# Four seven-product chunks instead of three in three feed-forward parts, and weights split 1024 columns at a time

## The chip, the cores and the metric

The kernel runs on one core of a Trainium2 chip. The metric is the time of one execution in device microseconds; lower is better. The core has five instruction streams that run side by side and meet through semaphores: PE (TensorE: matmuls and transposes), DVE (VectorE), ACT (ScalarE), POOL (GpSimd) and SP (SyncE, which issues the DMAs here). Each stream runs its instructions in the order of the program.

## The reference

The model is a trunk of two layers over 256 rows of width 1024. Every layer has a half-step feed-forward part, a mixer, and a second half-step feed-forward part:

```python
D_MODEL = 1024; SEQ = 256; DEPTH = 2; D_FF = 2816
def swiglu(h, w_gate, w_up, w_down):
    return (jax.nn.silu(h @ w_gate) * (h @ w_up)) @ w_down
for i in range(DEPTH):
    h = rmsnorm(x, ffn1_norm[i])
    x = x + 0.5 * swiglu(h, ffn1_w_gate[i], ffn1_w_up[i], ffn1_w_down[i])
    h = rmsnorm(x, mix_norm[i])
    proj = h @ w_in[i]          # q_s | k_s | v_s | q_m
    ...
    # i even: chunked attention with a relative bias; i odd: differential attention
    # with rotary q and k; both: cross attention into mem with 4 heads
    ...
    x = x + jnp.concatenate([o_s, o_m], axis=-1) @ w_out[i]
    h = rmsnorm(x, ffn2_norm[i])
    x = x + 0.5 * swiglu(h, ffn2_w_gate[i], ffn2_w_up[i], ffn2_w_down[i])
return x
```

All arrays are float32.

## The kernel before

The rows are two tiles of 128 (tb = 0 and 1). A float32 product is made of three matmuls on operands that were split in a high and a low piece: hi·hi, lo·hi and hi·lo. The function `dense` issues these three (L416, L419, L422), each with 128 rows and 512 columns.

The weights come in 164 chunks of 128x2048 float32, 1 MB each. `loader` (L281) issues their DMAs on SP's queue into three buffers called `raw`. `split_hi` (L321) makes the high piece on ACT by a cast, `hi<-raw`; `split_lo` (L340) makes the low piece on DVE by a subtraction, `lo<-raw,hi`. Both work on 512 columns in one instruction, so four instructions on each engine make a chunk. There are four hi and four lo buffers; a matmul that is done frees them.

The feed-forward part (`ffn`) has 11 groups of 256 hidden columns. Each group takes two chunks of gate and up weights into two PSUM banks `gu`. Then ACT applies silu (L526), DVE multiplies (L529) and transposes (L537, `hb`), a DMA writes that to DRAM (L543, `hd`) and another reads it back turned (L548, `hr`); ACT and DVE split it into `ht` (L557, L559). Then come 11 chunks of down weights, c = 0 to 10. Chunks 0 to 7 are used in turn. The last three (`SPLIT`) are used by quarters, first both column halves of the first row tile, then of the second; this is called the split run below. After each quarter `finish` adds the sum into x (L499), and PE's transposes (`xtp`), DVE and ACT make the next part's input from it (y L460, xh L463, xl L465).

In some down chunks the 8 block products of 128x128 by 128x512 are replaced by seven. The table `SEVEN` names them by layer and part: none in the first part of layer 0, chunks 1, 4, 6 in its second part and in the first part of layer 1, and 1, 4, 7 in the last. Such a chunk needs four sums of weight blocks on DVE (L334, `wsum`), seven splits instead of four on each engine, sums of the blocks of h (L573, `sf`) and their splits (L582 on ACT, L586 on DVE, `h7`), and four PSUM banks m1, m5, m6, m7, which are added up and put into x after the last such chunk (`seven_sums`: L617, L611, L606, `msum`). It spans two hi and two lo buffers. `seven_forms` of the third such chunk and of any later one waits in the plan until the second of them is at work.

The order of instructions on each engine is set when the program is written: `Flow` keeps a clock for each engine with a cost for each operation, and threads (loader, split_hi, split_lo, evac, ffn and so on) take their turn by that clock. `calm_a` and `calm_v` hold a split back until its engine is free in the plan. The chip sees only the resulting order and the semaphores.

In layer 1's mixer POOL and DVE share the rotary embedding: POOL multiplies by the sine table (L1038, two instructions), DVE by the cosine table (L1041, `m`) and DVE adds the two (L1045); PE then transposes the sum (`qktp`). Other names of the mixer: `pj` the input projection, `hss` and `v` sums of squares and their scaling, `qkn` the normed q and k, `pe` and `PT` the attention's weights, `oT` its output.

Of the kernel before, what the change touches and what calls it, by code (L numbers as in the profile page):

```python
# [12 lines left out]
F32 = mybir.dt.float32  # L13
# [7 lines left out]
P = 128  # L21
# [5 lines left out]
NG = FF // 256  # L27
# [115 lines left out]
def kernel(  # L143
# [96 lines left out]
    class Chunk:  # L240
        def __init__(self, parts):
            self.parts = parts
            self.raw = self.hi = self.lo = None
            self.arrive = self.early = None
            self.seven = False
            self.hit = [None] * 7
            self.lot = [None] * 7
            self.tt = [None] * 4
            self.uses = 0

        def part(self, lo, q):

            t = (self.lo if lo else self.hi)
            if self.seven:
                t, q = t[q // 4], q % 4
            return t[:, q * 512:(q + 1) * 512]

    chunks = []
# [5 lines left out]

    def add_chunk(parts, uses=8):
        c = Chunk(parts)
        c.uses = uses
        c.index = len(chunks)
        chunks.append(c)
        return c  # L270

    def loader():
        for i, c in enumerate(chunks):
            yield lambda: raw_left[0] > 0
            raw_left[0] -= 1
            c.raw = wraw.tile([P, 2048], F32, tag="raw", name=f"raw{i}")
            c.block = lambda q, c=c: c.raw[:, q * 512:(q + 1) * 512] if not c.seven else c.raw[:, (0, 2, 3)[q] * 512:
                                                                                          (1, 3, 4)[q] * 512]
# [26 lines left out]
    def split_hi():  # L305
        for i, c in enumerate(chunks):
            n = 2 if c.seven else 1
            yield lambda: c.raw is not None and hl_left[0] >= n
            hl_left[0] -= n
            yield c.early or c.arrive  # L310
            c.hi, c.lo = ([whl.tile([P, 2048], F32R, tag=x, name=f"{x}{i}_{j}") for j in range(n)] for x in ("hi", "lo"))
            if not c.seven:
                c.hi, c.lo = c.hi[0], c.lo[0]
            for q in range(7 if c.seven else 4):
                if q == 2:
                    yield c.arrive
                if c.seven and q >= 3:
                    yield lambda: c.tt[q - 3] is not None
                    yield c.tt[q - 3]
                yield calm_a(i)  # L320
                nc.scalar.copy(out=c.part(0, q), in_=c.block(q))  # L321
                c.hit[q] = flow.act(512)

    def split_lo():
        for i, c in enumerate(chunks):
            if c.seven:
                yield lambda: c.hi is not None and g2.left >= 6
                yield c.arrive
                r = [c.raw[:, q * 512:(q + 1) * 512] for q in range(4)]
                t = [g2.take([P, 512], F32, "wsum") for _ in range(4)]  # L330
                c.block = lambda q, r=r, t=t: ([r[0], r[2], r[3]] + t)[q]
                for j, x, y in ((0, r[1], r[0]), (1, r[3], t[0]), (2, r[3], r[1]), (3, r[2], t[1])):
                    yield calm_v(i)
                    nc.vector.tensor_sub(t[j], x, y)  # L334
                    c.tt[j] = flow.dve(512)
            for q in range(7 if c.seven else 4):
                yield lambda: c.hit[q] is not None
                yield c.hit[q]
                yield calm_v(i)
                nc.vector.tensor_sub(c.part(1, q), c.block(q), c.part(0, q).bitcast(F32))  # L340
                c.lot[q] = flow.dve(512)
                if q == 3:
                    raw_left[0] += 1
            if c.seven:
                g2.give(4)
# [16 lines left out]
    SEVEN = {(0, 1): (), (0, 2): (1, 4, 6), (1, 1): (1, 4, 6), (1, 2): (1, 4, 7)}  # L362
# [9 lines left out]

    def plan_ffn(l, nm, wg, wu, wd):
        gu = []
        for g in range(NG):
            ids = []
            for c in range(2):
                pieces = 2 if len(chunks) < 2 else 1
                a = cols4(wg[l], c, g * 256, 256, 0, pieces)
                b = cols4(wu[l], c, g * 256, 256, 256, pieces)  # L380
                ids.append(add_chunk([q for ab in zip(a, b) for q in ab]))
            gu.append(ids)
        plan[l, nm, "gu"] = gu
        dn = []
        for c in range(NG):
            dn.append(add_chunk(turned2(wd[l], c)))
            if c in SEVEN[l, nm]:
                dn[-1].seven, dn[-1].uses = True, 7
        plan[l, nm, "dn"] = dn
# [19 lines left out]
    def dense(ps, xh, xl, ready, c, need, sl, start, stop):  # L409
# [5 lines left out]
        wh, wl = (c.part(0, need), c.part(1, need)) if sl is None else (sl(c.hi), sl(c.lo))  # L415
        nc.tensor.matmul(out=ps, lhsT=xh, rhs=wh, start=start, stop=False)  # L416
        flow.pe(T_MM)
        flow.step()
        nc.tensor.matmul(out=ps, lhsT=xh, rhs=wl, start=False, stop=False)  # L419
        flow.pe(T_MM)  # L420
        flow.step()
        nc.tensor.matmul(out=ps, lhsT=xl, rhs=wh, start=False, stop=stop)  # L422
        c.uses -= 1
        if c.uses == 0:
            hl_left[0] += 2 if c.seven else 1
        return flow.pe(T_MM)
# [13 lines left out]
    class Xt:  # L440
        def __init__(self):
# [6 lines left out]
            self.done = [0, 0]  # L448

    def prep_half(xt, tb, hf, gc, wait=0.0):  # L450
# [15 lines left out]
        g2.give()  # L466
# [44 lines left out]
    def ffn(l, nm, xt, gc_next):  # L511
# [5 lines left out]
        def evac(g, ps, end):  # L517
# [3 lines left out]
            for tb in range(2):  # L521
# [11 lines left out]
                banks.give()  # L533
# [57 lines left out]
        def seven(c, ms):  # L591
# [3 lines left out]
            for q, j, m in ((0, 0, 0), (1, 1, None), (2, 6, None), (3, 3, 1), (4, 4, 2), (5, 5, 3), (6, 2, None)):  # L595
                ps = ms[m] if m is not None else acc.ps[q // 6][q // 2 % 2 if q < 6 else 0]
                t = dense(ps, ht[0][:, j], ht[1][:, j], lambda: htt[c], dn[c], q, None,
                          first and m is not None, last and m is not None)
# [41 lines left out]
        for g, ids in enumerate(plan[l, nm, "gu"]):  # L640
            flow.until(banks.has(2))
            ps = [bank(f"gu{tb}", (P, 512)) for tb in range(2)]
            end = [None, None]
            flow.spawn(evac(g, ps, end))
            order = [(tb, c) for tb in range(2) for c in range(2)] if g == 0 and (l, nm) != (0, 1) else \
                    [(tb, c) for c in range(2) for tb in range(2)]
            for tb, c in order:
                for k in range(4):
                    kk = 4 * c + k
                    t = dense(ps[tb], xt.h[tb][:, kk, :], xt.l[tb][:, kk, :], lambda: xt.t[tb][kk], ids[c], k,  # L650
                              lambda w: k4(w)[:, k, :], kk == 0, kk == KT - 1)
                if c == 1:
                    end[tb] = t
        flow.until(banks.has(4))
        acc = Acc()
        nxt = None if gc_next is None else Xt()
        dn = plan[l, nm, "dn"]

        def down(c, k, tb, hf):
# [4 lines left out]
                         lambda w: k2(w)[:, k, sl], c == 0 and k == 0, c == NG - 1 and k == 1)  # L664
# [145 lines left out]
    def memory_kv(l):  # L810
# [46 lines left out]
        for tb in range(2):  # L857
            for c in range(2):
                for k in range(4):
# [3 lines left out]
                              lambda w: k4(w)[:, k, :], kk == 0, kk == KT - 1)  # L863
# [117 lines left out]
    def mixer(l, xt, gc_next):  # L981
# [23 lines left out]
        def proj(i, evac):  # L1005
            flow.until(banks.has(2))
            ps = [bank(f"pj{tb}", (P, 512)) for tb in range(2)]
            for tb in range(2):
                for c in range(2):
                    for k in range(4):  # L1010
                        kk = 4 * c + k
                        t = dense(ps[tb], xt.h[tb][:, kk, :], xt.l[tb][:, kk, :], lambda: xt.t[tb][kk],
                                  plan[l, "in"][i][c], k, lambda w: k4(w)[:, k, :], kk == 0, kk == KT - 1)
# [357 lines left out]
        nxt = Xt()  # L1371
        ids = plan[l, "out"]

        def outp(i, k, tb, hf):
# [6 lines left out]
                         lambda w: k2(w)[:, k, sl], i == 0 and k == 0, i == 3 and k == 1)  # L1381
# [116 lines left out]
```

## Time and profile before

| | us |
|---|---|
| median of three executions | 964.88 |
| the three | 964.7, 964.88, 967.41 |
| the profiled execution | 964.95 |
| its span, first to last instruction | 963.2 |
| PE busy | 954.8 (99%) |
| DVE busy | 745.0 (77%) |
| ACT busy | 567.9 (59%) |
| POOL busy | 60.5 (6%) |

Rows of the profile give the line of the kernel (L340), the engine, the operation, what is written and read by the program's names (`lo<-raw,hi`), the shape, and how many. In the groups the numbers behind the bar are the busy time in us and the mean of one in ns, and behind the next bar the idle time just before them and what ended it. In a timeline the first number is the start in us and the second how long it took; in square brackets is the idle time before. PEld is the load of weights into the array, which overlaps PE. Matmuls overlap one another in the records, so that their rate is read from start to start.

### The profile page before, as it was taken

How to read it: one execution, taken by the hardware profiler on the slowest of the kernel's cores; microseconds unless marked ns; L12 is line 12 of the kernel's file. 1: busy time of each engine (PE TensorE's matmuls, PEld its weight loads, DVE VectorE, ACT ScalarE, POOL GpSimd, SP SyncE). 2: the span in 40 equal slices, each digit the busy share in tenths (PEclk: the TensorE clock that was granted, in tenths of full speed). 3: DMA queues.
4: the chain of work that ended last, by engine and by line, in shares of the span. 5: the costliest groups of instructions: out<-in, count | busy, mean ns of one | idle time of the engine just before them, and what ended most of it. 6: DMA issues, size and time to landing. Idle time of an engine off the chain costs nothing.

```text
span 963.2 us, 13464 instructions
## 1 busy us (share of the span) xinstructions
PE 954.8 (99%) x4525; PEld 783.9 (81%) x4525; DVE 745.0 (77%) x1569; ACT 567.9 (59%) x1215; POOL 60.5 (6%) x65
## 2 busy tenths in 40 slices
PE   8999999999999999999999999999999999999998
PEld 7888888888777888888888888888787788888886
DVE  6777777788777877759986775797989886776785
ACT  6655555666676655545645555565677765554551
POOL 0000000021210000000000000000343100000000
PEclk9999999999999999999999999999999999999999
DMA  8988877486525479766568777666641468777661
GB/s 282 328 267 285 250 263 246 145 272 208 176 88 175 154 224 284 235 229 205 184 208 254 247 245 220 212 202 219 207 143 44 134 196 283 232 254 225 215 190 44
DMA packets 169295, 204.04 MB, mean 212 GB/s; under 512 B 9673, under 2 KB 144394, under 8 KB 169226
## 3 DMA queue, kind: packets, MB, share of 16 engines
q1 hardware_dynamic: 169226, 203.18, 66.0%
q8 instruction: 35, 0.57, 0.2%
q14 instruction: 34, 0.28, 0.1%
HBM read 188.99 MB, written 14.16 MB: 211 GB/s over the span
## 4 chain that ended last, share of the span: by engine, by line
PE 94%; DVE 3%; ACT 1%; DMA 1%; SPq 0%; issue 0%; ACTq 0%
PE gu L422 17%; PE gu L416 17%; PE gu L419 17%; PE acc L416 9%; PE acc L422 9%; PE acc L419 9%; PE pj L422 3%; PE pj L416 3%; PE pj L419 3%; PE xtp L429 1%; PE ptp L429 1%; PE S L1139 1%; PE AV L1220 1%; PE m L422 1%; PE m L419 1%; PE m L416 1%
## 5 line engine op out<-in xcount | busy, mean ns | idle before, releaser
L340 DVE TENSOR_TENSOR lo<-raw,hi 128x512 fp32r<-128x512 f32 x647 | 413.7, 684 | 103.9 <-ACT hi L321 100.0
L321 ACT CAST hi<-raw 128x512 fp32r<-128x512 f32 x647 | 361.7, 618 | 219.0 <-PE gu L422 123.6
L422 PE MATMUL gu<-hi,xl 128*128 128x512 f32 x704 | 274.3, 390 | 0.0
L416 PE MATMUL gu<-hi,xh 128*128 128x512 f32 x704 | 274.1, 389 | 0.0
L419 PE MATMUL gu<-lo,xh 128*128 128x512 f32 x704 | 274.0, 389 | 0.0
L422 PEld LDWEIGHTS gu<-hi,xl 128*128 128x128 f32 x704 | 132.2, 188 | 27.4
L419 PEld LDWEIGHTS gu<-lo,xh 128*128 128x128 f32 x704 | 132.2, 188 | 27.3
L416 PEld LDWEIGHTS gu<-hi,xh 128*128 128x128 f32 x704 | 132.2, 188 | 27.3
L416 PE MATMUL acc<-hi,ht 128*128 128x512 f32 x280 | 109.6, 391 | 0.0
L422 PE MATMUL acc<-hi,ht 128*128 128x512 f32 x280 | 109.2, 390 | 0.0
L419 PE MATMUL acc<-lo,ht 128*128 128x512 f32 x280 | 109.1, 390 | 0.0
L422 PE MATMUL pj<-hi,xl 128*128 128x512 f32 x160 | 64.5, 403 | 0.0
L419 PE MATMUL pj<-lo,xh 128*128 128x512 f32 x160 | 63.6, 397 | 0.0
L416 PE MATMUL pj<-hi,xh 128*128 128x512 f32 x160 | 63.5, 397 | 0.0
L422 PEld LDWEIGHTS acc<-hi,ht 128*128 128x128 f32 x280 | 52.6, 188 | 11.0
L419 PEld LDWEIGHTS acc<-lo,ht 128*128 128x128 f32 x280 | 52.6, 188 | 10.7
L416 PEld LDWEIGHTS acc<-hi,ht 128*128 128x128 f32 x280 | 52.6, 188 | 10.7
L526 ACT ACTIVATE sil<-gu,xr 128x256 f32<-128x256 f32 x88 | 41.5, 472 | 28.6 <-PE gu L422 28.6
L559 DVE TENSOR_TENSOR ht<-hr,ht 128x512 fp32r<-128x512 f32 x35 | 24.1, 687 | 32.2 <-ACT ht L557 32.2
L529 DVE SCALAR_TENSOR_TENSOR h<-gu,xr,sil 128x256 f32<-128x256 f32 x88 | 42.2, 479 | 5.8 <-ACT sil L526 4.5
L557 ACT CAST ht<-hr 128x512 fp32r<-128x512 f32 x35 | 21.6, 618 | 41.9 <-DMA hr<-hd 41.8
L436 POOL TENSOR_TENSOR xr<-v,nhalf 128x1 f32<-128x1 f32 x12 | 8.4, 698 | 502.3 <-DVE v L434 502.3
(191 smaller groups left out, 1069.0 us busy)
## 6 DMA issues: line engine op xcount, KB each, us to landing
raw<-in_ffn_w_down_dram SPq DMA_DIRECT2D x176, 256.0 KB, 4.1
raw<-in_ffn_w_gate_dram SPq DMA_DIRECT2D x86, 512.0 KB, 4.3
raw<-in_ffn_w_up_dram SPq DMA_DIRECT2D x86, 512.0 KB, 5.5
raw<-in_w_in_dram SPq DMA_DIRECT2D x32, 512.0 KB, 4.1
hd<-hb SPq DMA_DIRECT2D x44, 256.0 KB, 2.3
hr<-hd SPq DMA_DIRECT2D x44, 256.0 KB, 5.3
raw<-in_w_out_dram SPq DMA_DIRECT2D x8, 1024.0 KB, 5.0
raw<-in_w_mem_kv_dram SPq DMA_DIRECT2D x4, 1024.0 KB, 5.4
```

Of the source, the lines that this page charges most:

```text
L321: nc.scalar.copy(out=c.part(0, q), in_=c.block(q))
L340: nc.vector.tensor_sub(c.part(1, q), c.block(q), c.part(0, q).bitcast(F32))
L416: nc.tensor.matmul(out=ps, lhsT=xh, rhs=wh, start=start, stop=False)
L419: nc.tensor.matmul(out=ps, lhsT=xh, rhs=wl, start=False, stop=False)
L422: nc.tensor.matmul(out=ps, lhsT=xl, rhs=wh, start=False, stop=stop)
L429: nc.tensor.transpose(out=dst, in_=src, identity=flip if flipped else ident)
L526: nc.scalar.activation(sil, ps[tb][:, 0:256], AF.Silu, scale=xt.r[tb])
L529: nc.vector.scalar_tensor_tensor(out=h, in0=ps[tb][:, 256:512], scalar=xt.r[tb], in1=sil, op0=ALU.mult, op1=ALU.mult)
L557: nc.scalar.copy(out=hi, in_=src)
L559: nc.vector.tensor_sub(lo, src, hi.bitcast(F32))
L1139: nc.tensor.matmul(out=ss[e][:, pr, :nk], lhsT=q[rows, pr, :], rhs=k[rows, pr, :], start=i == 0, stop=i == len(passes) - 1)
L1220: nc.tensor.matmul(out=av[64 * e:64 * e + 64, pr, :], lhsT=vsrc(kb, pr, e), rhs=pts[e][:, pr, kb, :], start=(kb == 0), stop=(kb == nb - 1))
```

## The change

Two things change. `SEVEN` becomes (1, 3, 5, 7) in the three parts that have such chunks. And a weight split takes 1024 columns at a time instead of 512, on ACT and on DVE, in all chunks but the first two. In a seven-product chunk one raw block is split alone (512), two that lie side by side together (1024), and the four sums alone (512 each). The sums no longer wait for a hi buffer in the plan, but for the raw chunk alone, and the raw buffer is given back in the plan after all splits of the chunk instead of after the fourth. For this the class `Chunk` is divided into a raw part and an `Item` that holds its splits as a list of units.

The changed kernel also has code for products of pairs of gate and up groups. Its table `PAIR` is None for every part, so this code issues nothing.

```diff
+    class Item:
+        def __init__(self, raws, uses=8):
...
+            w = 1 if len(items) < 2 else 2
+            self.units = [(self.own(q, w), q, w, None) for q in range(0, 4, w)]
...
     def split_hi():
...
-            for q in range(7 if c.seven else 4):
...
-                nc.scalar.copy(out=c.part(0, q), in_=c.block(q))
-                c.hit[q] = flow.act(512)
+            for src, q, w, dep in it.units:
...
+                nc.scalar.copy(out=it.part(0, q, w), in_=src())
+                t = flow.act(512 * w)
+                it.hit[q:q + w] = [t] * w
     def split_lo():
...
-                yield lambda: c.hi is not None and g2.left >= 6
-                yield c.arrive
...
+                yield lambda: all(r.raw is not None for r in it.raws) and g2.left >= it.takes + 2
+                yield max(r.arrive for r in it.raws)
...
-                nc.vector.tensor_sub(c.part(1, q), c.block(q), c.part(0, q).bitcast(F32))
-                c.lot[q] = flow.dve(512)
-                if q == 3:
-                    raw_left[0] += 1
+                nc.vector.tensor_sub(it.part(1, q, w), src(), it.part(0, q, w).bitcast(F32))
+                t = flow.dve(512 * w)
+                it.lot[q:q + w] = [t] * w
+            raw_left[0] += it.frees
...
-    SEVEN = {(0, 1): (), (0, 2): (1, 4, 6), (1, 1): (1, 4, 6), (1, 2): (1, 4, 7)}
+    SEVEN = {(0, 1): (), (0, 2): (1, 3, 5, 7), (1, 1): (1, 3, 5, 7), (1, 2): (1, 3, 5, 7)}
+    PAIR = {(0, 1): None, (0, 2): None, (1, 1): None, (1, 2): None}
...
+    def seven_item(it):
+        r = [it.own(q) for q in range(4)]
+        t = lambda j: lambda: it.t[j]
+        it.n, it.uses, it.takes, it.gives = 2, 7, 4, 4
+        it.sums = [(r[1], r[0]), (r[3], t(0)), (r[3], r[1]), (r[2], t(1))]
+        it.units = [(r[0], 0, 1, None), (it.own(2, 2), 1, 2, None)] + [(t(j), 3 + j, 1, j) for j in range(4)]
```

The order on three places follows. The number behind a name tells its chunk (76) and then a running number that differs between the two kernels; `x4` stands for four like instructions in a row.

DVE, in the down run of layer 0's second part, before: chunks 3 and 4 (76 and 77 in the program's count), where chunk 77 is a seven-product one, and the forms of the third such chunk.

```order
L340 TENSOR_TENSOR lo76_0_4540<-raw76_4356,hi76_0_4539 128x512 x4
L334 TENSOR_TENSOR wsum_4586<-raw77_4460 128x512
L334 TENSOR_TENSOR wsum_4587<-raw77_4460,wsum_4586 128x512
L334 TENSOR_TENSOR wsum_4588<-raw77_4460 128x512
L334 TENSOR_TENSOR wsum_4589<-raw77_4460,wsum_4587 128x512
L340 TENSOR_TENSOR lo77_0_4583<-raw77_4460,hi77_0_4581 128x512
L559 TENSOR_TENSOR ht_4601<-hr_4559,ht_4601 128x512
L340 TENSOR_TENSOR lo77_0_4583<-raw77_4460,hi77_0_4581 128x512 x2
L340 TENSOR_TENSOR lo77_0_4583<-wsum_4586,hi77_0_4581 128x512
```

The same place on DVE after the change, where chunk 76 is the seven-product one (`L344` is the split, `L657` a sum of blocks of h, `L670` its split); the rows begin with the last splits of its sums.

```order
L344 TENSOR_TENSOR lo76_1_4280<-wsum_4231,hi76_1_4278 128x512
L643 TENSOR_TENSOR ht_4300<-hr_4268,ht_4300 128x512
L657 TENSOR_TENSOR sf_4324<-hr_3789 128x128
L657 TENSOR_TENSOR sf_4324<-sf_4324,hr_3789 128x128
L657 TENSOR_TENSOR sf_4324<-hr_3789 128x128
L657 TENSOR_TENSOR sf_4324<-hr_3789,sf_4324 128x128
L657 TENSOR_TENSOR sf_4331<-hr_3981 128x128
L657 TENSOR_TENSOR sf_4331<-sf_4331,hr_3981 128x128
L657 TENSOR_TENSOR sf_4331<-hr_3981 128x128
L657 TENSOR_TENSOR sf_4331<-hr_3981,sf_4331 128x128
L344 TENSOR_TENSOR lo76_1_4280<-wsum_4232,hi76_1_4278 128x512
L670 TENSOR_TENSOR h7_4323<-hr_3789,h7_4322 128x256
```

The sums of blocks of h for the third and the fourth seven-product chunk now stand in one group ahead of the last split of chunk 76, and their splits behind it; before, one chunk's forms came at a time.

DVE, in the first part of layer 1, before: the end of the plain chunk 7 (113 in the program's count) and the last three, 114 to 116, with the sums of products (`L611`, `L606`) among them.

```order
L340 TENSOR_TENSOR lo113_0_6363<-raw113_6241,hi113_0_6362 128x512 x4
L340 TENSOR_TENSOR lo114_0_6388<-raw114_6279,hi114_0_6387 128x512 x4
L340 TENSOR_TENSOR lo115_0_6425<-raw115_6369,hi115_0_6424 128x512
L606 SCALAR_TENSOR_TENSOR x0_85<-msum_6431,x0_85 128x512
L611 TENSOR_TENSOR msum_6431<-msum_6431,m6_6157 128x512
L340 TENSOR_TENSOR lo115_0_6425<-raw115_6369,hi115_0_6424 128x512
L611 TENSOR_TENSOR msum_6432<-msum_6431,m5_6156 128x512
```

After the change (`L690` and `L695` are the sums), from the last split of chunk 113 on, which is now a seven-product one.

```order
L344 TENSOR_TENSOR lo113_1_5987<-wsum_5979,hi113_1_5985 128x512
L344 TENSOR_TENSOR lo114_0_6016<-raw114_5947,hi114_0_6015 128x1024 x2
L344 TENSOR_TENSOR lo115_0_6031<-raw115_5971,hi115_0_6030 128x1024 x2
L690 SCALAR_TENSOR_TENSOR x0_85<-msum_6073,x0_85 128x512
L695 TENSOR_TENSOR msum_6073<-msum_6073,m6_5762 128x512
L344 TENSOR_TENSOR lo116_0_6071<-raw116_6035,hi116_0_6070 128x1024
L695 TENSOR_TENSOR msum_6074<-msum_6073,m5_5761 128x512
L690 SCALAR_TENSOR_TENSOR x0_85<-msum_6074,x0_85 128x512
L344 TENSOR_TENSOR lo116_0_6071<-raw116_6035,hi116_0_6070 128x1024
```

The sums now stand among the splits of chunk 116, the last of the part, where they stood among those of chunk 115.

DVE, at the start of layer 1's mixer, before: the rotary embedding of the first block.

```order
L713 SCALAR_TENSOR_TENSOR qkn_6733<-pj0_6626,xr_6103,hf_6695 128x512
L340 TENSOR_TENSOR lo121_0_6708<-raw121_6623,hi121_0_6707 128x512
L1041 TENSOR_TENSOR m1_6757<-qkn_6733,ropeC_107 128x512
L340 TENSOR_TENSOR lo122_0_6737<-raw122_6663,hi122_0_6736 128x512
L707 TENSOR_REDUCE hss_6768<-sq_6746 128x8
L434 TENSOR_SCALAR v_6771<-hss_6768 128x8
L1045 TENSOR_TENSOR m1_6757<-m1_6757,m2_6756 128x512
L340 TENSOR_TENSOR lo122_0_6737<-raw122_6663,hi122_0_6736 128x512 x3
```

After the change (`L894` is qkn, `L1222` and `L1226` are the multiply and the add).

```order
L894 SCALAR_TENSOR_TENSOR qkn_6328<-pj0_6220,xr_5711,hf_6284 128x512
L344 TENSOR_TENSOR lo122_0_6321<-raw122_6248,hi122_0_6320 128x1024
L888 TENSOR_REDUCE hss_6342<-sq_6332 128x8
L514 TENSOR_SCALAR v_6345<-hss_6342 128x8
L1222 TENSOR_TENSOR m1_6348<-qkn_6328,ropeC_107 128x512
L1226 TENSOR_TENSOR m1_6348<-m1_6348,m2_6347 128x512
L344 TENSOR_TENSOR lo122_0_6321<-raw122_6248,hi122_0_6320 128x1024
L894 SCALAR_TENSOR_TENSOR qkn_6379<-pj1_6221,xr_5712,hf_6344 128x512
```

The split, the sum of squares and its scaling, which stood between the multiply and the add, now stand ahead of both.

Over the whole program the matmuls of 128x512 fall by 9, the splits `lo<-raw,hi` on DVE go from 647 of 512 columns to 20 of 512 and 312 of 1024, and the casts `hi<-raw` on ACT likewise; splits of weight sums go from 36 to 48 on each engine and the weight sums from 36 to 48. SP and POOL issue as many instructions as before; on SP some of the DMAs of `hd` and `hr` move past one or two loads of `raw`.

More of the change, by code (lines that the diff above doesn't have):

```diff
@@ L263, with add_raw @@
     at = [0]
+    def add_raw(parts):
+        chunks.append(Chunk(parts))
+        return chunks[-1]
     def add_chunk(parts, uses=8):
[L266 to L270, printed above, removed]
+        return Item([add_raw(parts)], uses)
     def loader():
@@ L305, in split_hi @@
     def split_hi():
[L306 to L313, printed above, removed]
-            for q in range(7 if c.seven else 4):
+        for i, it in enumerate(items):
+            yield lambda: hl_left[0] >= it.n and all(r.raw is not None for r in it.raws)
+            hl_left[0] -= it.n
+            yield max(r.early or r.arrive for r in it.raws)
+            it.hi, it.lo = ([whl.tile([P, 2048], F32R, tag=x, name=f"{x}{i}_{j}") for j in range(it.n)]
+                            for x in ("hi", "lo"))
+            for src, q, w, dep in it.units:
@@ L383, in plan_ffn @@
         plan[l, nm, "gu"] = gu
+        plan[l, nm, "work"] = [w for w in work if w not in ("11", "12", "22", "21")]
+        if pair is not None:
+            plan[l, nm, "pair"] = made
         dn = []
@@ L414, in dense @@
         at[0] = max(at[0], c.index)
-        wh, wl = (c.part(0, need), c.part(1, need)) if sl is None else (sl(c.hi), sl(c.lo))
+        wh, wl = c.part(0, need), c.part(1, need)
         nc.tensor.matmul(out=ps, lhsT=xh, rhs=wh, start=start, stop=False)
@@ L424, in dense @@
         if c.uses == 0:
-            hl_left[0] += 2 if c.seven else 1
+            hl_left[0] += c.n
         return flow.pe(T_MM)
@@ L465, in prep_half @@
         nc.vector.tensor_sub(xt.l[tb][:, ks, :], y, xt.h[tb].bitcast(F32)[:, ks, :])
-        g2.give()
+        if xt.keep:
+            xt.y[tb, hf] = y
+        else:
+            g2.give()
         t = flow.dve(512)
@@ L638, in seven_sums, with plain_chunk @@
             g2.give(2)
[L640 to L647, printed above, removed]
+        open_ = {}
+        def plain_chunk(g, c, tbs):
+            if g not in open_:
+                flow.until(banks.has(2))
+                open_[g] = [bank(f"gu{tb}", (P, 512)) for tb in range(2)], [None, None]
+                flow.spawn(evac(g, *open_[g]))
+            ps, end = open_[g]
+            for tb in tbs:
@@ new lines, in product @@
+        def product(m):
+            name, left = {"m1": ("b11", (0, 0)), "m5": ("t1", 0), "m7": ("t3", 2), "m6": ("t2", 1), "m3": ("b22", 3),
+                          "m2": ("b21", (0, 1)), "m4": ("t4", (1, 1))}[m]
+            flow.until(banks.has())
+            pb[m] = bank("pair_" + m, (P, 512))
+            if m == "m1":
+                flow.spawn(pair_sums())
+                for e in range(2):
+                    flow.spawn(evac(pair + e, pps[e], pend[e], (g2, g2)))
+            for k in range(4):
+                if isinstance(left, int):
+                    flow.until(lambda: xt.ft[left] is not None)
+                    f = xt.fm[left]
+                    fh, fl, ready = f[:, 0, k, :], f[:, 1, k, :], lambda: xt.ft[left]
+                else:
+                    tb, kk = left[0], 4 * left[1] + k
+                    fh, fl, ready = xt.h[tb][:, kk, :], xt.l[tb][:, kk, :], lambda: xt.t[tb][kk]
+                t = dense(pb[m], fh, fl, ready, pit[name], k, k == 0, k == 3)
+            mt[m] = t
+            if m == "m3":
+                g4.give(4)
@@ L654, in ffn @@
+        if pair is not None:
+            flow.spawn(pair_forms())
+        work = list(plan[l, nm, "work"])
+        if (l, nm) != (0, 1):
+            for tb in range(2):
+                for c in range(2):
+                    plain_chunk(0, c, (tb,))
+            work = work[2:]
+        for w in work:
+            if isinstance(w, str):
+                product(w)
+            else:
+                plain_chunk(*w, range(2))
         flow.until(banks.has(4))
         acc = Acc()
-        nxt = None if gc_next is None else Xt()
+        nxt = None if gc_next is None else Xt(nm == 2 and PAIR[l + 1, 1] is not None)
```

210 lines of the change are left out of this document (156 added, 54 removed).

## The prediction

> **What bounds the kernel now.** I read the page first (busy time, chain, groups), then the windows, the waits, and the timelines of the places that the change touches.
>
> ```profile
> span 963.2 us, 13464 instructions
> PE 954.8 (99%) x4525; PEld 783.9 (81%) x4525; DVE 745.0 (77%) x1569; ACT 567.9 (59%) x1215; POOL 60.5 (6%) x65
> PE 94%; DVE 3%; ACT 1%; DMA 1%; SPq 0%; issue 0%; ACTq 0%
> L340 DVE TENSOR_TENSOR lo<-raw,hi 128x512 fp32r<-128x512 f32 x647 | 413.7, 684 | 103.9 <-ACT hi L321 100.0
> L321 ACT CAST hi<-raw 128x512 fp32r<-128x512 f32 x647 | 361.7, 618 | 219.0 <-PE gu L422 123.6
> ```
>
> PE is busy for 99% of the span, and the chain that ended last is PE for 94%. DVE and ACT spend most of their time on the weight splits, and each waits on others: ACT's idle time is ended mostly by PE, which is PE giving back hi and lo buffers. The windows give it by stage: steady gate/up work, a down run (layer 0's second part, from its first seven-product pass on), and layer 1's mixer.
>
> ```profile
> 820.00:880.00 60.00, 60.00 (x266) 49.73 (x265) 42.73 (x80) 32.09 (x63) 0.00 (x0) 1.00 0.78 243
> 443.10:478.50 35.40, 35.40 (x158) 29.31 (x157) 31.59 (x55) 22.93 (x43) 0.00 (x0) 1.00 0.67 215
> 684.00:750.00 66.00, 64.45 (x359) 51.13 (x359) 60.02 (x136) 46.42 (x130) 29.33 (x25) 1.00 0.41 136
> 750.00:790.00 40.00, 39.56 (x227) 31.88 (x226) 34.62 (x73) 28.18 (x73) 2.32 (x3) 1.00 0.49 152
> ```
>
> Columns: length, then busy us and count of PE, weight loads, DVE, ACT, POOL; granted clock; DMA share; GB/s. The feed-forward windows leave PE no gap at a granted clock of 1.00, though DVE is at 31.59/35.40 = 89% in the down run. Only the mixer leaves PE idle: 1.55 + 0.44 = 1.99 us. PE's own waits name them:
>
> ```profile
> PE ptp L429 <- DVE pe L1266: 0.7, 2, 0.6
> PE acc L416 <- DVE oT L1127: 0.4, 1, 0.4
> PE qktp L429 <- DVE m L1045: 0.4, 1, 0.4
> PE qktp L429 <- ACT PT L1153: 0.4, 1, 0.4
> ```
>
> So only two things shorten the span: fewer matmuls, or smaller mixer waits. Faster splits in the feed-forward parts buy slack.
>
> **The matmuls removed.** One seven-product chunk has 7 products of three matmuls where a plain one has 8: three fewer. Three parts get one more each: 9 fewer 128x512 matmuls. A matmul's record lasts 0.39 us, but they overlap; what counts is start to start:
>
> ```profile
> 819.76 0.39 PE L416 MATMUL gu<-hi,xh 128*128 128x512 f32 x1
> ...
> 829.97 0.39 PE L416 MATMUL gu<-hi,xh 128*128 128x512 f32 x1
> ```
>
> 45 starts lie between them: 10.21/45 = 0.227 us. Nine are 2.04 us, all on the path, provided that nothing else starts to wait.
>
> **What the three new seven-product chunks add on DVE and ACT.** Each adds four weight sums, three 512-wide splits more on both engines (seven for four), and forms of h.
>
> ```profile
> 457.15 0.28 DVE L573 TENSOR_TENSOR sf<-hr 128x128 f32<-128x128 f32 x1
> 457.46 0.29 DVE L573 TENSOR_TENSOR sf<-sf,hr 128x128 f32<-128x128 f32 x1
> 457.68 0.28 DVE L573 TENSOR_TENSOR sf<-hr 128x128 f32<-128x128 f32 x1
> 457.88 0.28 DVE L573 TENSOR_TENSOR sf<-hr,sf 128x128 f32<-128x128 f32 x1
> 458.08 0.62 DVE L586 TENSOR_TENSOR h<-hr,h 128x256 fp32r<-128x256 f32 x2
> 458.85 0.69 DVE L586 TENSOR_TENSOR h<-sf,h 128x512 fp32r<-128x512 f32 x1
> 463.79 2.49 DVE L340 TENSOR_TENSOR lo<-wsum,hi 128x512 fp32r<-128x512 f32 x4
> 463.75 2.18 ACT L321 CAST hi<-raw 128x512 fp32r<-128x512 f32 x4 [0.38 <-ACT hi L321]
> L582 ACT CAST h<-hr x18: 293/348/406, 353.3 to 924.6; 128x256 fp32r<-128x256 f32 x9, 128x128 fp32r<-128x128 f32 x9
> L582 ACT CAST h<-sf x9: 614/620/622, 354.1 to 924.8; 128x512 fp32r<-128x512 f32 x9
> ```
>
> DVE runs 512-wide work at (2.49 − 0.69)/3 = 0.60 us start to start, ACT at (2.18 − 0.62)/3 = 0.52. Forms take 4 x 0.20 + 0.53 (the two L586 rows, without their 0.09 of overlap with the next) + 0.60 = 1.93 us on DVE, in place of one 0.60 split: +1.33. DVE gains 12 x 0.60 (sums) + 9 x 0.60 (splits) + 3 x 1.33 = 16.6 us, ACT 9 x 0.52 and some 0.5 a set of forms, about 6.
>
> **The wide splits.** 624 of the 512-wide splits become 312 of 1024 on each engine. No row shows that width, so its price is bounded: from above by two single ones (1.20 on DVE, 1.04 on ACT), from below by the slope alone. DVE: (684 − 284)/(512 − 128) = 1.04 ns an element, so 512 more are 0.53: 1.13 start to start, saving 0.07 a pair, about 20 us in all. ACT: (620 − 406)/256 = 0.84, so 0.52 + 0.43 = 0.95, saving 0.09 a pair, some 29 us. I take these. In net DVE is about 4 us lighter and ACT 23. On the path: zero in the feed-forward parts, since there PE hides the splits already. The cost of width is that a block's first half is ready one half later, about 0.5 us each on ACT and DVE; in gate/up PE reads buffers filled long before, and 60.00 of 60.00 busy leaves nothing to gain.
>
> **The down runs: is the cover still there?** The passes now alternate. One seven-product pass and one plain one take PE 45 x 0.227 = 10.2 us. DVE needs for them 2.4 (sums) + 0.6 + 1.13 + 2.4 + 2 x 1.13 = 8.8 us. From the second chunk to the eighth that is 4 x 6.5 + 3 x 2.3 plus two sets of forms (3.9) and one split of ht (0.6): 37.4 us of DVE for 35.3 of PE. It starts ahead:
>
> ```profile
> 470.99 0.39 PE L416 MATMUL m<-hi,h 128*128 128x512 f32 x1
> ```
>
> This matmul reads the first wsum block of the third seven-product chunk, whose split above was done at 463.79 + 0.69 = 464.5: 6.5 us ahead. Off that come 2.1 us of deficit and up to 2 us of forms in one piece, since the forms of the third and fourth now stand in one group: 2 to 4 us are left, and PE does not wait. SP's loads of raw wait for a DVE split anyway, and hd and hr move past one or two loads only, so I put the queues at zero. Behind the last seven-product pass the six sums of products now fall into the split run in all three parts. In the last part they do so already:
>
> ```profile
> 942.87 0.69 DVE L606 SCALAR_TENSOR_TENSOR x<-msum,x 128x512 f32<-128x512 f32 x1
> ...
> 944.62 1.28 DVE L340 TENSOR_TENSOR lo<-raw,hi 128x512 fp32r<-128x512 f32 x2
> 942.62 0.39 PE L422 MATMUL acc<-hi,h 128*128 128x512 f32 x1
> 942.85 0.39 PE L416 MATMUL acc<-hi,ht 128*128 128x512 f32 x1
> ```
>
> PE passes from the seven products to the plain ones at 0.23 us, its usual step. I take 0, with bounds of 0 and +1.5 (in the two parts where it is new, one split 0.53 longer and 0.2 of queueing each).
>
> **The mixer of layer 1.** Its first wait:
>
> ```profile
> 688.88 1.23 DVE L1041 TENSOR_TENSOR m<-qkn,ropeC 128x512 f32<-128x512 f32 x1
> 690.03 1.22 DVE L340 TENSOR_TENSOR lo<-raw,hi 128x512 fp32r<-128x512 f32 x1
> 691.97 0.39 PE L419 MATMUL pj<-lo,xh 128*128 128x512 f32 x1
> 692.79 0.63 PE L429 MATMUL qktp<-ident,m 128*128 128x128 f32 x4 [0.43 <-DVE m L1045]
> L1038 POOL TENSOR_TENSOR m<-qkn,ropeS x12: 730/829/1669, 688.5 to 737.1; 128x256 f32<-128x256 f32 x12
> ```
>
> Start to start it is 0.82 us instead of 0.23: 0.59 lost where the record shows 0.43 idle. By that ratio the mixer's 1.99 us cost 2.7. The rotary multiply and add (L1041, L1045) had a split of 1.22 us between them; in the changed order they stand together, and one wide split follows. I take this wait as gone, −0.6, and the others as unchanged: a wide split delays ready work by up to 0.5 more, but there is 15 x 0.07 = 1 us less to do. Bounds: −2.7 (all waits gone) and +2.7 (five waits each 0.54 longer).
>
> [...]
>
> **Sum.** The profiled execution took 964.95 us (span 963.2 and 1.75 around it), the median of the runs is 964.88: the same within 0.1. 964.95 − 2.04 − 0.6 + 0 = 962.3 us.
>
> **The rivals.**
> - B, relief: less work for ACT and DVE empties nearly all mixer waits. 964.95 − 2.04 − 2.7 = 960.2. For it: what of the chain is not PE is DVE 3% and ACT 1%. Against: DVE is busy 60.02 of 66.00 and gets only 1 us less. [...]
> - C, the gain is lost again: the hand-over to the split run, or to the next part, makes PE wait 0.7 us in each of three parts. 964.95 − 2.04 + 2.1 = 965.0. For it: lead there is thin, and six sums and wide splits share DVE. Against: the last part shows no such gap.
> [...]
>
> **How the numbers follow.** Chances: A (forecast, 961.3 to 963.6) 0.54, B 0.24, C 0.14, D 0.08. About 0.3%, 2.9 us, is what a measurement of this kernel can tell from no change, so faster means below 962.0, slower above 967.8. A lies just above the lower line; I put 0.13 of its 0.54 below it. Faster 0.13 + 0.24 = 0.37; same 0.41 + 0.14 = 0.55; slower 0.08. The range 960.0 to 965.5 holds A, C and the nearer part of B.
>
> **What would show it.** Right: nine fewer PE matmuls at the same 0.227 us; wide rows near 1.22 us on DVE and 1.05 on ACT; down-run windows with PE full; PE's wait for m gone. [...]

## The result, and the profile after

The changed kernel takes 974.37 us (median of four, 973.06 to 976.6) against 964.79: 1.0095 of the time before, with a 95% interval of 1.0082 to 1.0107. It is slower by 9.6 us between the medians, where 2.6 less were forecast. The profiled execution took 973.06, 8.1 above that of the kernel before (964.95).

The page of the changed kernel, busy time, chain and the two groups of splits:

```profile
span 971.3 us, 12884 instructions
PE 956.3 (98%) x4516; PEld 780.8 (80%) x4516; DVE 736.1 (76%) x1296; ACT 541.2 (56%) x918; POOL 64.1 (7%) x65
PE 71%; DVE 14%; DMA 8%; ACT 3%; issue 2%; SPq 2%; ACTq 0%; DVEq 0%
L344 DVE TENSOR_TENSOR lo<-raw,hi 128x1024 fp32r<-128x1024 f32 x312 | 374.0, 1220 | 59.9 <-ACT hi L326 56.6 <-DMA raw<-in_ffn_w_down_dram 2.5 <-DMA raw<-in_ffn_w_gate_dram 0.3
L326 ACT CAST hi<-raw 128x1024 fp32r<-128x1024 f32 x312 | 318.2, 1048 | 114.5 <-PE gu L502 66.6 <-PE pj L502 13.5 <-DMA raw<-in_ffn_w_down_dram 8.8
```

What was counted and priced came as forecast: nine matmuls fewer (4525 to 4516), 1.22 us for a wide split on DVE and 1.05 on ACT; DVE is 9 us lighter where 4 were worked out. But the chain is no longer PE's alone: some 29% of it is now DVE, DMA, ACT and queues. The waits say where. In the order of the fence: PE's new wait, then those of ACT and DVE for `ht`, the turned h of a plain group; the same two were 41.8 and 32.2 us before. These are sums over the whole program: of DVE's 97.4 us only 13.0 lie in the three down runs that have seven-product chunks. Most of the others lie in the gate/up parts, where PE waits for nothing (110.00 of 110.00 us busy from 320 to 430).

```profile
PE acc L499 <- DVE lo L344: 7.6, 8, 1.6
ACT ht L641 <- DMA hr<-hd: 138.7, 28, 7.6
DVE ht L643 <- ACT ht L641: 97.4, 28, 5.6
```

The windows of the three down runs, first of the kernel before, then of the changed one:

```profile
437.50:496.80 59.30, 59.30 (x269) 49.09 (x268) 51.17 (x90) 33.04 (x64) 0.55 (x1) 1.00 0.64 204
616.90:676.10 59.20, 59.20 (x269) 48.99 (x268) 50.92 (x90) 34.34 (x66) 0.55 (x1) 1.00 0.63 204
901.20:959.00 57.80, 57.80 (x257) 47.82 (x255) 43.73 (x76) 25.88 (x49) 0.00 (x0) 1.00 0.47 150
```

```profile
437.30:498.90 61.60, 59.54 (x266) 48.31 (x265) 55.20 (x86) 33.64 (x51) 0.00 (x0) 1.00 0.62 196
619.00:681.70 62.70, 59.50 (x266) 48.24 (x265) 55.45 (x86) 35.62 (x53) 0.55 (x1) 1.00 0.61 193
906.70:967.10 60.40, 57.95 (x254) 46.98 (x252) 48.51 (x75) 27.00 (x40) 0.00 (x0) 1.00 0.43 144
```

Each run is 2 to 3.5 us longer though it has three matmuls fewer, and DVE has 4 to 5 us more to do in it. The rest of the program did not change: gate/up takes 119.9 us in each of the last three parts (121.3 against 121.4 in the first), and layer 1's mixer 104.8 us against 104.9 (first matmul of its projections to the first of the next part).

The first of these down runs. Rows of SP, DVE and ACT of the changed kernel, with the wait in square brackets:

```profile
435.80 9.03 SPq L288 DMA_DIRECT2D raw<-in_ffn_w_down_dram  x8
444.93 0.53 SPq L627 DMA_DIRECT2D hd<-hb  x1
449.26 0.36 SPq L632 DMA_DIRECT2D hr<-hd  x1
442.08 0.44 DVE L621 STREAM_TRANSPOSE hb<-h 128x256 f32<-128x256 f32 x1
446.68 1.89 DVE L344 TENSOR_TENSOR lo<-wsum,hi 128x512 fp32r<-128x512 f32 x3
452.02 0.62 ACT L641 CAST ht<-hr 128x512 fp32r<-128x512 f32 x1 [4.94 <-DMA hr<-hd]
452.67 0.69 DVE L643 TENSOR_TENSOR ht<-hr,ht 128x512 fp32r<-128x512 f32 x1 [4.11 <-ACT ht L641]
```

`hb` of the last group is ready at 442.5, but its DMA `hd` stands on SP behind eight loads of `raw`, and leaves at 444.9; the way back, `hr`, leaves at 449.3 and has landed at 452.0. ACT's cast of `ht` and DVE's split of it stand in their queues ahead of the last split of chunk 3 (76 in the program's count), of the forms and of all chunks behind. So DVE is idle for 4.1 us, although this `ht` is needed only by the last chunk, some 29 us later (its first matmul starts at 481.7): the work that could have filled the time stands behind it in DVE's order. From 452.7 on DVE works without a gap up to 480.6, and it is still late:

```profile
457.93 0.39 PE L496 MATMUL acc<-hi,ht 128*128 128x512 f32 x1
458.70 0.50 PE L499 MATMUL acc<-lo,ht 128*128 128x512 f32 x1 [0.38 <-DVE lo L344]
...
482.79 0.40 PE L496 MATMUL acc<-hi,ht 128*128 128x512 f32 x1
484.75 0.50 PE L499 MATMUL acc<-lo,ht 128*128 128x512 f32 x1 [1.56 <-DVE lo L344]
```

PE waits for a lo at chunk 4 (458.7) and again for the last chunk of the split run (484.75), where it loses 1.96 − 0.23 = 1.73 us at one matmul. In the kernel before, the same wait at the same place was short:

```profile
440.71 0.34 SPq L543 DMA_DIRECT2D hd<-hb  x1
443.09 2.55 SPq L281 DMA_DIRECT2D raw<-in_ffn_w_down_dram  x4
445.74 0.54 SPq L548 DMA_DIRECT2D hr<-hd  x1
449.86 0.62 ACT L557 CAST ht<-hr 128x512 fp32r<-128x512 f32 x1 [2.17 <-DMA hr<-hd]
450.52 0.69 DVE L559 TENSOR_TENSOR ht<-hr,ht 128x512 fp32r<-128x512 f32 x1 [0.88 <-ACT ht L557]
```

There `hd` stood ahead of the loads of chunk 5, and DVE came to `ht` only after the sums of the seven-product chunk 4.

### The profile page after: what moved, and what is told of

It is laid out like the page before. It is cut to its first block, busy times and chain, and to the rows that moved or that the text cites. A ratio compares the mean times of both kernels' runs of the same rounds, so it can differ in the third digit from the quotient of the medians.

```text
span 971.3 us, 12884 instructions
## 1 busy us (share of the span) xinstructions
PE 956.3 (98%) x4516; PEld 780.8 (80%) x4516; DVE 736.1 (76%) x1296; ACT 541.2 (56%) x918; POOL 64.1 (7%) x65
## 4 chain that ended last, share of the span: by engine, by line
PE 71%; DVE 14%; DMA 8%; ACT 3%; issue 2%; SPq 2%; ACTq 0%; DVEq 0%
PE gu L502 14%; PE gu L499 14%; PE gu L496 14%; DVE lo L344 7%; PE acc L499 5%; PE acc L502 5%; PE acc L496 5%; DMA raw<-in_ffn_w_down_dram 3%; PE pj L496 3%; PE pj L502 3%; PE pj L499 3%; ACT hi L326 2%; DMA hd<-hb 2%; DMA hr<-hd 2%; DVE wsum L338 2%
## 5 line engine op out<-in xcount | busy, mean ns | idle before, releaser
L344 DVE TENSOR_TENSOR lo<-raw,hi 128x1024 fp32r<-128x1024 f32 (+1 forms) x332 | 386.7, 1187 | 59.9 <-ACT hi L326 56.6
L326 ACT CAST hi<-raw 128x1024 fp32r<-128x1024 f32 (+1 forms) x332 | 329.1, 1022 | 128.1 <-PE gu L502 66.6
L499 PE MATMUL acc<-lo,ht 128*128 128x512 f32 x256 | 101.1, 395 | 7.7 <-DVE lo L344 7.6
L496 PE MATMUL acc<-hi,ht 128*128 128x512 f32 x256 | 100.0, 391 | 0.0
L502 PE MATMUL acc<-hi,ht 128*128 128x512 f32 x256 | 99.9, 390 | 0.0
L643 DVE TENSOR_TENSOR ht<-hr,ht 128x512 fp32r<-128x512 f32 x32 | 22.0, 687 | 97.4 <-ACT ht L641 97.4
L499 PEld LDWEIGHTS acc<-lo,ht 128*128 128x128 f32 x256 | 48.1, 188 | 21.0 <-DVE lo L344 11.5
L496 PEld LDWEIGHTS acc<-hi,ht 128*128 128x128 f32 x256 | 48.1, 188 | 10.0
L502 PEld LDWEIGHTS acc<-hi,ht 128*128 128x128 f32 x256 | 48.1, 188 | 9.5
L516 POOL TENSOR_TENSOR xr<-v,nhalf 128x1 f32<-128x1 f32 x12 | 11.5, 957 | 486.5 <-DVE v L514 486.5
```

Source lines behind the costliest of these rows:

```text
L326: nc.scalar.copy(out=it.part(0, q, w), in_=src())
L344: nc.vector.tensor_sub(it.part(1, q, w), src(), it.part(0, q, w).bitcast(F32))
L516: nc.gpsimd.tensor_tensor(out=dst, in0=v[:, :n], in1=nhalf[:, :n], op=ALU.pow)
L643: nc.vector.tensor_sub(lo, src, hi.bitcast(F32))
```

## The experiments

Three theories stood at the start. T1: the wait for `ht` at the head of ACT's and DVE's queues takes the time. T2: four alternating seven-product chunks are too much for DVE, whatever it waits for. T3: the first half of a wide split comes too late. Each was timed beside the kernel before on its own chip (965.0 to 965.4 us there). For each I read from PE's timeline how long the three down runs took, from the last gate/up matmul to the first matmul of what follows (in the last, to the last matmul). Without any wait they should take 0.68 us (three matmuls) less than before: 58.80, 58.80 and 57.12.

| kernel | time, us | ratio to before, 95% | down runs, us | DVE idle before the last group's ht in each |
|---|---|---|---|---|
| before | 965.4 | | 59.48, 59.48, 57.80 | 0.88, 1.29, 1.54 |
| changed | 974.37 | 1.0082 to 1.0107 | 61.75, 62.86, 60.44 | 4.11, 4.64, 4.28 |
| late ht | 964.29 | 0.998 to 1.0001 | 58.77, 59.93, 57.12 | none |
| hd first | 968.43 | 1.002 to 1.0043 | 59.79, 60.84, 58.54 | 1.92, 2.35, 2.11 |
| narrow | 976.13 | 1.0089 to 1.0127 | 63.68, 64.34, 60.34 | 3.92, 3.26, 3.52 |
| narrow, late ht | 964.75 | 0.9986 to 1.001 | 59.26, 59.64, 57.59 | none |
| old chunks, wide | 966.41 | 0.9989 to 1.0011 | 59.45, 59.45, 57.80 | 1.65, 2.24, 2.50 |
| chunks 1, 3, 5 | 971.6 | 1.0054 to 1.0079 | 61.20, 61.86, 58.43 | 4.18, 4.33, 4.11 |

**The late ht.** One edit moves the cast and the split of the last group's `ht` back; on DVE no other row changes place but two splits, the last of chunk 3 and the first of chunk 4, which now stand earlier among the forms. The orders of PE and SP stay.

```diff
             src = hr.rearrange("p a (c j) -> p c a j", c=4)
...
+            if g == NG - 1 and sv:
+                yield lambda: prog[0] >= 4
             yield g4.has()
             ht = g4.take([P, 2, 4, P], F32R, "ht")
```

> The changed kernel with one edit: the split of the last group's ht (used only in the split run) is placed behind the start of the fifth down chunk in the plan, so that ACT and DVE do not stand behind its DMA at the third chunk. Work and sums are the same. Three theories for the 10.4 us that PE lost in the three down runs. T1, a wait at the head of ACT's and DVE's queues (ht for its DMA, 4.1 to 4.6 us of DVE idle in each run): the waits of PE on lo go and the time is 962 to 965. T2, capacity (four alternating seven-product chunks are more than DVE can do in the run, whatever it waits for): PE still waits, 969 to 973. T3, width (the first half of a 1024-wide split comes too late): unchanged, 972 to 975.

Measured: 964.29 us, 10.1 below the changed kernel and inside the range given for T1. Against the kernel before it is 1.1 us less, which the interval does not tell from nothing. In two down runs PE lost nothing, and these are shorter than before by the three matmuls. DVE is still nearly full there; the window of the first run from its first seven-product pass on:

```profile
442.90:479.00 36.10, 36.10 (x161) 29.91 (x160) 35.14 (x55) 24.63 (x36) 0.00 (x0) 1.00 0.69 217
```

PE 36.10 of 36.10, DVE 35.14 of 36.10, 97%. So the work fits, barely, and T2 and T3 fall as causes by themselves. A single wait is left, in layer 1's first part, whose down run takes 1.13 us more than 58.80:

```profile
661.55 0.50 PE L499 MATMUL acc<-lo,ht 128*128 128x512 f32 x1 [0.85 <-DVE lo L344]
```

**hd first.** Only SP's order changes against the changed kernel: `hd` of the last group stands ahead of the loads of chunk 5. No row of PE, DVE or ACT changes place, so this run prices the wait alone.

```diff
-            yield lambda: raw_left[0] > 0
+            yield lambda: raw_left[0] > 0 and (c.hold is None or hd_out[c.hold])
...
+            if c == 5 and SEVEN[l, nm]:
+                chunks[-1].hold = (l, nm)
+                hd_out[l, nm] = False
...
+            if g == NG - 1:
+                hd_out[l, nm] = True
             yield flow.now + 3.0
```

> The changed kernel with one edit on SP's queue: the DMA hd of the last group stands ahead of the four loads of down chunk 5, as it did before the change, instead of behind them; the order on ACT and DVE is the same. T1: hd leaves some 2.3 us earlier, so DVE's idle before ht shrinks from 4.1-4.6 to 1.5-2.5 us, and PE loses less by about as much in each run: 964 to 968. T2 and T3: within 1 us of the changed kernel, 972 to 975.

Measured: 968.43, 0.4 above the range given for T1 and far below that of T2 and T3. The wait shrinks to about half, and the loss by 1.9 to 2.0 us a run:

```profile
442.84 0.34 SPq L631 DMA_DIRECT2D hd<-hb  x1
443.28 2.68 SPq L289 DMA_DIRECT2D raw<-in_ffn_w_down_dram  x4
446.05 0.54 SPq L638 DMA_DIRECT2D hr<-hd  x1
450.78 0.69 DVE L649 TENSOR_TENSOR ht<-hr,ht 128x512 fp32r<-128x512 f32 x1 [1.92 <-ACT ht L647]
```

So the wait has a price: between one of 4.11 and one of 1.92 us the loss in the first run goes from 61.75 − 58.80 = 2.95 to 0.99, 0.89 us for each us of wait; the other two runs give 0.88. By this slope the first 0.8 us are absorbed in the first run (0.99 / 0.89 = 1.1 us of the 1.92 show). The third gives 0.5 in the same way, and the second 1.3, if the 1.13 us that the late `ht` leaves there are taken off first. This is an estimate from two kernels: DVE had about 1 us of lead to give.

**Narrow splits.**

```diff
-            w = 1 if len(items) < 2 else 2
+            w = 1
...
-        it.units = [(r[0], 0, 1, None), (it.own(2, 2), 1, 2, None)] + [(t(j), 3 + j, 1, j) for j in range(4)]
+        it.units = [(r[0], 0, 1, None), (it.own(2), 1, 1, None), (it.own(3), 2, 1, None)] + [(t(j), 3 + j, 1, j) for j in range(4)]
```

> The changed kernel with all splits 512 columns wide again; chunks 1, 3, 5, 7 stay. In the plan hd of the last group then stands ahead of the loads of chunk 5, and ht one split earlier. T1: the wait for ht is about 2 us instead of 4.3, so that part of the loss goes: 964 to 968. T2: DVE has more to do (0.07 us more for a pair of splits, some 1 us in a down run): 973 to 977. T3: PE waits for no lo: 962 to 964.

Measured: 976.13, the slowest of all and inside the range given for T2. I had mispriced the wait: `hr` leaves earlier here (445.67), but `ht` also stands one split sooner on DVE, so the wait is 3.3 to 3.9 us and not 2. The `ht` of the group before, which costs the changed kernel nothing in these runs, stops DVE for 0.55, 2.50 and 1.00 us more. PE loses 4.9 and 5.5 us in the first two runs and 3.2 in the third, but not all of it to waits. Just behind PE's last wait in the first two runs matmuls start 0.43 us apart instead of 0.23, at a granted clock of 0.53 and 0.51; the changed kernel has 1.00 in the same place. The windows are two of the narrow kernel, then one of the changed one:

```profile
486.30:489.30 3.00, 3.00 (x7) 2.42 (x8) 2.97 (x6) 0.95 (x2) 0.00 (x0) 0.53 0.45 117
670.50:673.50 3.00, 3.00 (x7) 2.42 (x8) 2.96 (x6) 0.60 (x2) 0.00 (x0) 0.51 0.65 152
```

```profile
484.70:487.70 3.00, 2.95 (x14) 2.40 (x15) 2.97 (x5) 1.72 (x2) 0.00 (x0) 1.00 0.98 313
```

Seven steps from start to start take 3.0 us there (486.29 to 489.31) and 1.74 in the changed kernel (484.75 to 486.49). That is some 1.3 us in each of the two runs; without it the loss would be some 3.6, 4.2 and 3.2 us, near that of the changed kernel. Why the clock fell is not shown. All five executions of this kernel have a mean granted clock of 0.994 to 0.998, so each holds time below 1.00, and lying in T2's range is no proof of T2. T3 falls: without wide splits PE still waits for lo. The same kernel with the late `ht`:

> 512-wide splits, chunks 1, 3, 5, 7, and the late place of the last group's ht: both edits of before at once. It tells the wait for ht from the work. If the wait alone made the loss of the narrow kernel (976 us), the time is as with wide splits and the late ht, 964 to 966. If DVE's work is at its limit in the down runs, the narrow splits (0.07 us more for a pair, about 1 us in a run, and no room left) still make PE wait: 966 to 970.

Measured: 964.75, down runs 59.26, 59.64 and 57.59. The wait made nearly all of the loss. What narrow splits leave is about 0.5 us in the first and third run, which wide ones do not have; in the second run 0.84 are left, where wide ones leave 1.13. The `ht` of the group before stops DVE here too, for 0.74, 1.42 and 0.90 us, so the 0.5 is not the price of width alone: the wide splits are worth at most that.

**Old chunks, wide splits.** `SEVEN` is (1, 4, 6), (1, 4, 6), (1, 4, 7) again.

> The changed kernel with wide splits and the old chunks (1, 4, 6 twice and 1, 4, 7). hd and hr of the last group both stand behind loads here, so the wait for ht should be as long as in the changed kernel (4 us or more), but DVE has about 4 us less to do in each run. T1: the wait meets more slack, part of the loss stays or none: 963 to 968. T2: no loss, 963 to 965. T3: loss at the hand-over to the split run, 966 to 972.

Measured: 966.41, ratio 0.9989 to 1.0011, and the down runs are those of the kernel before to 0.03 us. ACT stands 4.5 to 5.3 us before `ht`, but DVE comes there later (it has the sums of chunk 4 first), and is idle for 1.65 to 2.50 us, with enough lead behind. There is no loss at the hand-over. With the old chunks, width changes nothing that PE sees.

**Chunks 1, 3, 5.**

> The changed kernel with wide splits, ht in its early place, and chunks 1, 3, 5 instead of 1, 3, 5, 7: the same order around the wait for ht, but one set of forms, sums and three splits less behind it (about 5.5 us of DVE work a run). If the loss is the wait plus the work less the lead, the wait of 4 us stays in the trace and PE loses little: 964 to 966 (six matmuls a part as before the change). If the wait is enough by itself, PE loses 2 to 3 us a part as in the changed kernel: 971 to 975.

Measured: 971.6. One seven-product chunk less behind the wait, and the run still loses 1.7, 2.4 and 0.6 us against the 59.48, 59.48 and 57.80 that three seven-product chunks take without a wait. So the fourth chunk is not needed for a loss; it makes it larger, by 1.2 to 2.7 us a run. That the wait ahead of chunk 3's last split makes the loss here too is inferred from the late `ht`; chunks 1, 3 and 5 were not run with it.

**The hand-over in layer 1's first part.** ACT's table load for the mixer (1.28 us) and the copy `msum` stand there ahead of the last chunk's casts. The load moves to the fifth chunk (c = 4):

```diff
+            if nm == 1 and c == (4 if sv else SPLIT - 1):
+                table_hint(AF.Exp)
...
-        if nm == 1:
-            table_hint(AF.Exp)
```

> The late ht, and in layers' first parts ACT's table load for the mixer (1.28 us) moved from the hand-over to the split run up to the fifth down chunk. With the late ht alone PE still waited 0.9 us for a split of the last chunk in layer 1's first part, behind the table load and the sums of products. If the table load made that wait, it goes: 963 to 964, 0.5 to 1.2 below the late ht alone. If the sums among the splits made it, no change: 964 to 965.

Measured: 965.4, above both ranges, though the second down run is 58.80 us, the full gain. The edit also changed the plan: on DVE one more split now stands ahead of the first of the sums of products. And layer 1's mixer came out in another order, and took 107.1 us instead of 104.8. PE's waits there:

```profile
PE ptp L509 <- DVE pe L1384: 1.7, 1, 1.7
PE ptp L509 <- DVE qmn L896: 0.5, 1, 0.5
```

A third edit, which starts the sums of products only behind the last chunk's splits (`yield lambda: dn[NG - 1].lot[3] is not None` in `seven_sums`), came with the same mixer:

> As the one with the late ht and the moved table load, and the sums of products start only when the last chunk's splits stand ahead of them on DVE. If the sums made PE's last wait, it goes here: 963 to 964, a gain of 0.2 to 0.3% over the kernel before. Rival: x comes later, so the next part's input (xtp, xl) makes PE wait at its start, up to 1 us a part: 964 to 967.

Measured: 966.16, ratio 1.0 to 1.0019; the second run is 58.77, the mixer 107.15. The time lies in the rival's range, but through the mixer: the part behind each down run starts as before. In this pair of kernels the place of the sums makes no difference to PE.

**Late ht, table load at the seventh chunk (c = 6).** With the load here the orders on PE, DVE and ACT in layer 1's first part and its mixer are those of the late `ht` alone; only the load itself moves.

> The late ht, and the table load of layer 1's first part at the seventh down chunk: chosen because the order of PE and DVE in the mixer behind it is then the same as with the late ht alone (with the load at the fifth chunk the plan of the mixer came out differently and PE waited there 1.7 us for pe). If the table load made the 0.9 us wait at the hand-over and the mixer's order the loss behind it, the span is some 0.9 to 1.2 below the late ht alone: 960.5 to 961.2, a time of 962.3 to 963.2. Rival: the hand-over's wait comes from the sums of products: as the late ht alone, 963.7 to 964.5.

Measured: 964.01, ratio 0.9989 (0.998 to 0.9998), the only version clear of the kernel before, by 0.1%. The time lies in the rival's range. Its second down run is 59.27 and PE's last wait there 0.2 us; the mixer takes 104.82. So the table load made 0.66 of the 1.13 us; 0.47 stay with the load gone and the sums in their old place. Whether these belong to the sums is open: they went where one more split stood ahead of the sums. Its profiled execution started late (last section), so its span is not used. The old chunks with the late `ht`:

> The late ht and wide splits with the old chunks (1, 4, 6 twice and 1, 4, 7): beside the other kernel of this pair it prices the nine matmuls alone. If nothing else differs, it is 9 x 0.227 = 2.04 us slower than the other: 964.5 to 965.2, and the same as the kernel before. Rival: the mixer's plan comes out differently, and the difference is off by 1 us or more.

Measured: 965.43, ratio 0.9989 to 1.0011, 0.2 above the range and the same as the kernel before. The two differ by 1.42 us. 2.04 for nine matmuls less the 59.27 − 58.80 = 0.47 that the second run still loses is 1.57, which fits within the 0.1% or so that the intervals leave.

## Why the prediction was wrong

- **Nine matmuls, −2.04 us: right.** In the late `ht` the first and third runs are 0.71 and 0.68 us shorter than before; three matmuls are 0.68.
- **Prices of the wide splits and what they are worth in gate/up: right.** 1220 and 1048 ns against 1.22 and 1.05; gate/up 119.9 us in all kernels; width alone (old chunks, wide) 0.
- **Work of DVE in the down run: right in size.** By the prediction's prices chunks 3 to 7 with both sets of forms and the `ht` are 3 x 6.5 + 2 x 2.3 + 3.9 + 0.6 = 28.6 us. With the late `ht` DVE takes 29.3 us for them without a gap (442.69 to 471.97), and PE does not wait.
- **"I put the queues at zero": this step failed.** I saw that `hd` and `hr` move past a load or two, and the order that I showed has `ht` on DVE ahead of chunk 76's last split; I costed neither. One row of the order (`hd` behind the loads of chunk 5) and one of DVE (`ht` ahead of the last split) turned a wait of 0.9 to 1.5 us into one of 4.1 to 4.6. With a lead of about 1 us the three runs lost 2.95, 4.06 and 3.32: 10.3 us, which is all of the loss and the gain besides. The late `ht` took back 2.98, 2.93 and 3.32 of these, 9.2 us; the other 1.13 is the hand-over below.
- **The lead: "2 to 4 us are left" was too much.** It was counted from one chunk in the old trace, where DVE ran at 89%. The two kernels with the wait show about 1 us before PE waits.
- **Hand-over, 0 with bounds of 0 and +1.5: the size was within the bounds, in one part.** With the late `ht`, layer 1's first part lost 1.13 us. The table load on ACT, which I had not listed there, made 0.66 of it; what made the other 0.47 is open.
- **Mixer, −0.6: it was −0.07.** The wait for m fell from 0.43 to 0.20 us as the order promised. But the others did not stay as they were: the wait of 0.6 us for `pe` on DVE and two of 0.4 went, one of 0.7 us in `otp` for `pe` on ACT (L1433) and two of 0.3 came. PE's idle time there fell from 1.98 to 1.57 us, and the mixer's time still hardly moved.
- **Rival C named the right kind of loss (PE waits in each of three parts) and 2.1 us for it; it was five times that, and not for its reason: with the late `ht` the six sums and the wide splits still stand in the split run, and two of the three parts lose nothing.** B did not come: of PE's 1.98 us of idle time in the mixer 1.57 stayed. For D, the chance of 0.08, no run shows that POOL's multiplies grew: the twelve rotary ones took 11.3 us against 11.5 before, 738 ns at the median against 829. DVE's own rotary multiply took 679 to 1205 ns, the longest beside one of POOL's; before, 673 to 1228, and of those beside one of POOL's two took 1.23 and 1.22 us and two 0.68 and 0.69.

## What to carry to other kernels

DVE and ACT kept to the order of the program here: a cast and a split that waited for a DMA round trip (7.1 us from the issue of `hd` at 444.93 to the cast at 452.02) held up all that stood behind them, DVE for 4.1 us, though their result was needed only some 29 us later. So put the consumer of a slow round trip as late as its use allows. When a change fills an engine, as here from 89 to 97%, the lead that used to hide such waits can be gone; so every wait that was free in the old trace (0.9 to 1.5 us here) has to be priced again, and every DMA that moves past another in the queue with it. After a small edit of a kernel that plans its own order, look whether the plan changed elsewhere: here a better hand-over was paid for with 2.3 us in the mixer.

## What the runs showed beside this

The start of the program differed between the profiled executions, and the difference carried into the time: PE's first transposes waited for the DMA of x for 0.50 us in the changed kernel, for 0.87 us in the kernel before and for 3.15 us in the profile of the version with the load at the seventh chunk, whose execution took 967.46 against a median of 964.01. The first matmul of gate/up starts 2.2 us later there. The first gate/up part is some 1.9 us longer besides, 123.3 against 121.4: some of its first matmuls start 0.43 us apart, at a granted clock of 0.57, where the kernel before has 1.00.

```profile
8.58 0.66 PE L429 MATMUL xtp<-ident,x 128*128 128x128 f32 x4 [0.87 <-DMA x<-in_x_dram]
10.45 1.12 PE L509 MATMUL xtp<-ident,x 128*128 128x128 f32 x4 [3.15 <-DMA x<-in_x_dram]
```

From 13 to 17 us, first the kernel before, then that version:

```profile
13.00:17.00 4.00, 4.00 (x19) 3.31 (x18) 4.00 (x7) 2.74 (x7) 0.00 (x0) 1.00 1.10 348
13.00:17.00 4.00, 4.00 (x15) 3.14 (x14) 1.29 (x2) 2.13 (x4) 0.00 (x0) 0.57 1.08 343
```

For differences of 1 us the stages of two traces are therefore the better measure here than their spans.
